# The first MLP product of a decoder layer in pairs of tiles by Strassen's rule, with two sums of weights made by accumulating DMAs

## The chip, the cores and the metric

The kernel runs on one core of a Trainium2 chip. The metric is the device time of one execution in microseconds, the median of 3 runs. The core has TensorE (PE, matrix products, with a weight loader PEld beside it), VectorE (DVE), ScalarE (ACT), GpSimd (POOL), SyncE (SP) and 16 DMA engines. In this kernel SP issues nearly all DMAs; a DMA that POOL issues goes through another queue, called software_dynamic in the profile.

## The reference, cut to what matters

One layer with T=512 tokens, D=2048, D_FF=8192, all in float32. What stands ahead of the second half (an input projection, three mixers, an output projection) is not touched by the change.

```python
x = x + g1 * mix
h = rms_norm(x, norm2_g[l]) * (1.0 + sc2) + sh2
x = x + g2 * (jnp.square(jax.nn.relu(h @ w_mlp1[l])) @ w_mlp2[l])
return rms_norm(x, final_norm_g)
```

Here `sc2`, `sh2` and `g2` are sections of `c_act @ ada_w + ada_b`, vectors of 2048 elements each.

## The kernel before, in words

Every float32 matrix is split into a high part (a cast to the type float32r, on ScalarE) and a low part (the difference, on VectorE). A product of two matrices is three products on TensorE: high by high, low by high, high by low.

The hidden width of 8192 is cut into 64 tiles of 128 rows. The first MLP product `h @ w_mlp1` makes one tile after another, with all 512 tokens as the columns of a matmul. Tiles 0 to 6 are made together in a "wide" phase that goes along the contraction (k = 0 to 15) while `h2`, the normalised input, is still being made. Tiles 7 to 63 come out of `full_k`: 16 steps of k by 3 matmuls of 512 columns, 48 for a tile. Their weights come in four loads of 256 KB a tile through the class `Stream` (tiles `w_raw`), each split into `w_hi` (L135) and `w_lo` (L136).

A tile gets its squared ReLU (`relu2`). After every second tile the four quarters of the two tiles (each 128 x 256) are turned by four subtractions into the seven left factors of a Strassen rule, which the second MLP product uses already: `hx`, 128 x 7 x 256, at L1003 to L1006. They are split into `hx_hi` (L1009) and `hx_lo` (L1010) and written to DRAM in two DMAs of 896 KB (L1012, `hid_dram`). `hx`, `hx_hi` and `hx_lo` have two buffers each.

Between the tiles the kernel fits 16 pieces of `g2` (`ada_piece`: loads of 1 MB and two dots of 128 x 1024 on VectorE, L247), in tiles 7 to 21, and in tiles 8 to 11 `x1_tokens`: 64 transposes on TensorE, 16 copies on ScalarE and 16 DMAs.

Before the last two tiles a pool is closed, and the first two right factors of the second MLP product are loaded ahead, one of them already split. The second MLP product (L1028 to L1031) then takes seven products for each block, with `hs` (left factors) read back from `hid_dram` and `b` (weights, 512 KB a load) split at L975 and L976.

What runs ahead of what on an engine is decided by the order of the program and by the calls `issue_after` and `high_priority`; each engine, SP and POOL too, takes its instructions in order, so one that waits holds up those behind it.

## Time and profile before

| what | value |
|---|---|
| median of 3 runs | 2028.3 us (2026.03 to 2035.21) |
| the profiled execution | 2029.22 us, span 2027.5 us |
| mean granted TensorE clock | 0.994 |
| PE busy | 1981.5 us, 98% of the span, 9141 matmuls |
| DVE busy | 1490.1 us, 73% |
| ACT busy | 844.4 us, 42% |
| POOL busy | 9.8 us |
| DMA | 499.52 MB, mean 246 GB/s |

The share of an engine is an average over stages with different limits; the stretch that the change rewrites is that of tiles 14 to 63, 831.4 to 1385.1 us. The stretch 664.5 to 831.4 us holds the wide phase and tiles 7 to 13.

### The profile page before, as it was taken

To read this page: it belongs to the slowest core of one execution; us is meant where nothing else is said; L and a number is where in the kernel's file an instruction comes from. 1 tells how busy PE (TensorE), PEld (TensorE's weight loads), DVE (VectorE), ACT (ScalarE), POOL (GpSimd) and SP (SyncE) were. 2 spreads that over 40 slices of the span, in tenths; PEclk is the share of its full clock that TensorE was granted. 3 is DMA by queue.
4 is the path that set the end of the run, shared out by engine and by line. 5 is a ranking of instruction groups with operands and counts; after the bars stand their busy time and mean duration, and the time that the engine had idled before them with its cause. 6 is when DMAs were issued, how large, how long until landed. Compare 5 with 4: busy or idle time off the path is not lost.

```text
span 2027.5 us, 25042 instructions
## 1 busy us (share of the span) xinstructions
PE 1981.5 (98%) x9141; PEld 1626.3 (80%) x9141; DVE 1490.1 (73%) x2090; ACT 844.4 (42%) x1258; POOL 9.8 (0%) x17
## 2 busy tenths in 40 slices
PE   9999989999999999999999999999999999999996
PEld 7888977677888887777888888887888887888885
DVE  8998779779987897566444444446887787877778
ACT  5434347776423445323333333334333333433333
...
GB/s 383 296 309 174 247 184 162 182 146 222 273 333 230 92 125 330 278 292 309 216 166 200 179 166 198 180 168 287 333 326 317 309 274 273 345 294 306 310 233 207
DMA packets 217627, 499.52 MB, mean 246 GB/s; under 512 B 16696, under 2 KB 84864, under 8 KB 196640
## 3 DMA queue, kind: packets, MB, share of 16 engines
...
q14 instruction: 51, 0.42, 0.1%
HBM read 430.72 MB, written 67.14 MB: 246 GB/s over the span
## 4 chain that ended last, share of the span: by engine, by line
PE 72%; issue 15%; DMA 6%; DVE 5%; ACT 1%; SPq 0%; POOL 0%; DVEq 0%; ACTq 0%; POOLq 0%
PE ps_m L294 10%; PE ps_m L292 10%; PE ps_m L293 10%; PE ps_w L293 3%; PE ps_w L292 3%; PE ps_w L294 3%; PE ps_rot L1028 3%; PE ps_rot L1029 3%; PE ps_rot L1031 3%; PE ps_d L1031 2%; DMA ada<-in_ada_w 2%; PE ps_d L1028 2%; PE ps_d L1029 2%; PE ps_y L293 1%; PE ps_y L292 1%
## 5 line engine op out<-in xcount | busy, mean ns | idle before, releaser
L135 ACT CAST w_hi<-w_raw 128x512 fp32r<-128x512 f32 (+2 forms) x476 | 285.6, 603 | 582.1 <-PE ps_m L293 329.5
L136 DVE TENSOR_TENSOR w_lo<-w_raw,w_hi 128x512 fp32r<-128x512 f32 (+2 forms) x476 | 315.8, 668 | 260.6 <-ACT w_hi L135 255.9
L294 PE MATMUL ps_m<-h_hi,w_lo 128*128 128x512 f32 x912 | 357.0, 391 | 6.1 <-DVE w_lo L136 6.0
L292 PE MATMUL ps_m<-h_hi,w_hi 128*128 128x512 f32 x912 | 356.6, 391 | 0.0
L293 PE MATMUL ps_m<-h_lo,w_hi 128*128 128x512 f32 x912 | 355.8, 390 | 0.0
L975 ACT CAST v_hi<-b 128x2048 fp32r<-128x2048 f32 x96 | 183.5, 1913 | 299.0 <-PE ps_rot L1029 125.4
L976 DVE TENSOR_TENSOR v_lo<-b,v_hi 128x2048 fp32r<-128x2048 f32 x96 | 219.6, 2290 | 92.2 <-ACT v_hi L975 92.1
L247 DVE SCALAR_TENSOR_TENSOR ada<-ada,crow 128x1024 f32<-128x1024 f32 (+1 forms) x176 | 230.7, 1319 | 42.4 <-DMA ada<-in_ada_w 42.0
L294 PEld LDWEIGHTS ps_m<-h_hi,w_lo 128*128 128x128 f32 x912 | 171.6, 188 | 44.5 <-DVE w_lo L136 8.7
L1028 PE MATMUL ps_rot<-v_hi,hs 128*128 128x512 f32 x512 | 200.5, 392 | 3.8 <-issue 2.3
L292 PEld LDWEIGHTS ps_m<-h_hi,w_hi 128*128 128x128 f32 x912 | 171.7, 188 | 35.4 <-ACT w_hi L135 0.4
L293 PEld LDWEIGHTS ps_m<-h_lo,w_hi 128*128 128x128 f32 x912 | 171.6, 188 | 35.4
L1029 PE MATMUL ps_rot<-v_hi,hs 128*128 128x512 f32 x512 | 199.8, 390 | 0.0
L1028 PE MATMUL ps_d<-v_hi,hs 128*128 128x512 f32 x384 | 149.9, 390 | 4.1 <-DMA hs<-hid_dram 2.6
L1029 PE MATMUL ps_d<-v_hi,hs 128*128 128x512 f32 x384 | 149.4, 389 | 0.0
L1031 PE MATMUL ps_rot<-v_lo,hs 128*128 128x512 f32 x512 | 137.6, 391 | 0.0
L1028 PEld LDWEIGHTS ps_rot<-v_hi,hs 128*128 128x128 f32 x512 | 96.4, 188 | 26.0 <-issue 3.2
L1031 PEld LDWEIGHTS ps_rot<-v_lo,hs 128*128 128x128 f32 x512 | 96.7, 189 | 20.2
L1029 PEld LDWEIGHTS ps_rot<-v_hi,hs 128*128 128x128 f32 x512 | 96.4, 188 | 19.8
L1031 PE MATMUL ps_d<-v_lo,hs 128*128 128x512 f32 x384 | 102.9, 389 | 0.5 <-DVE v_lo L976 0.5
L1055 DVE TENSOR_TENSOR sum<-sum,ps_rot 128x512 f32<-128x512 f32 x112 | 76.2, 683 | 23.8 <-PE ps_rot L1031 23.7
L1028 PEld LDWEIGHTS ps_d<-v_hi,hs 128*128 128x128 f32 x384 | 72.1, 188 | 20.5 <-issue 2.3
...
## 6 DMA issues: line engine op xcount, KB each, us to landing
hs<-hid_dram SPq DMA_DIRECT2D x112, 1024.0 KB, 6.3
w_raw<-in_w SPq DMA_DIRECT2D x412, 256.0 KB, 3.1
b<-in_w SPq DMA_DIRECT2D x128, 512.0 KB, 6.6
...
ada<-in_ada_w SPq DMA_DIRECT2D x92, 512.0 KB, 5.0
hid_dram<-hx_hi SPq DMA_DIRECT2D x32, 896.0 KB, 4.8
hid_dram<-hx_lo SPq DMA_DIRECT2D x32, 896.0 KB, 5.2
...
```

The costliest lines, as they stand in the source:

```text
L135: self.split = nc.scalar.copy(hi, raw)
L136: self.in_order(lambda: nc.vector.tensor_sub(lo, raw, hi.bitcast(F32)))
L247: return V.scalar_tensor_tensor(w, w, 0.5, crow[:, sl], ALU.mult, ALU.mult, accum_out=acc[:, n:n + 1])
L292: PE.matmul(ps, lhsT=wh, rhs=pair[0], start=first, stop=False)
L293: PE.matmul(ps, lhsT=wh, rhs=pair[1], start=False, stop=False)
L294: PE.matmul(ps, lhsT=wl, rhs=pair[0], start=False, stop=last)
L975: S.copy(hi, raw)
L976: V.tensor_sub(lo, raw, hi.bitcast(F32))
L1028: PE.matmul(ps, lhsT=hs[:, 0, k, ts], rhs=hi[:, k], start=(first and k == 0), stop=False)
L1029: PE.matmul(ps, lhsT=hs[:, 1, k, ts], rhs=hi[:, k], start=False, stop=False)
L1031: PE.matmul(ps, lhsT=hs[:, 0, k, ts], rhs=lo[:, k], start=False, stop=(last and k == KP - 1))
L1055: V.tensor_add(d, d, s)
```

## The change: what it does

`N0 = 14`: tiles 0 to 13 are made as before, and tiles 14 to 63 in 25 pairs. A pair of tiles by 512 tokens by 2048 of contraction is cut in two in each of the three directions, and the two-by-two block product is made by 7 products instead of 8. One of them (`up_product`) is 8 steps of k (128 each) by 3 matmuls of 256 columns: 24 matmuls, 168 a pair, where a pair had 96 of 512 columns. The right-hand operands are halves of `h2` or sums of them (`next_sums`, 8 groups of 4 subtractions, 2 casts and 2 differences, made once, during tiles 8 and 9). The left-hand operands are quarters of the weights (512 KB each) or sums of them: `w22`, `w11` and `w21` are loaded by SP; `q4 = w12 + w22` and `q5 = w12 + w11` are each made by a plain DMA and an accumulating DMA on top of it, both issued by POOL; `w11 + q4` and `w21 + w11` are additions of 128 x 1024 on VectorE. Each of the 7 left-hand operands is split (128 x 1024, L1135 and L1136); the splits run two products ahead, with three buffers. The four quarters of the result are put together from the 7 sums in PSUM: two copies on ScalarE into `z3` (L1186, L1188) and four operations of 512 elements on VectorE (L1191, L1193, L1194, L1197), and ReLU and square are now two operations on ScalarE.

With it go other edits. Weight buffers (`w22`, `w11`, `w21`, `q4`, `q5`), `hx`, `hx_hi` and `z3` have one buffer each in the pair stage; the low part is written over `hx` itself (L1027). `h2` is computed in place on `x1`, so `x1_tokens` moves ahead into the wide phase. Of the 16 pieces of `g2`, 4 go into the wide phase, and the other 12 into 24 halves, one a pair (load L1170, dot L262). Nothing of the second MLP product is split or loaded before the pools of the pairs close; its first three splits stand behind them.

```diff
-    x = None
-    for n in range(NFT):
-        if n == NFT - 2:
-            groups_scope.close()
...
-            ahead.append(split(*next(todo)))
-            second = next(todo)
...
+        hi, lo = sums_hi[k], low.pop(0)
+        a, b = [x1[i // 4][:, i % 4] for i in (k, k + KH)]
+        h11, h21, h12, h22 = a[:, :HT], a[:, HT:], b[:, :HT], b[:, HT:]
+        V.tensor_sub(h11, h12, h11)
+        V.tensor_sub(h12, h12, h22)
+        V.tensor_sub(h22, h22, h11)
+        V.tensor_sub(h21, h21, h22)
+        for i, x in enumerate((a, b)):
+            S.copy(hi[:, i], x)
+            V.tensor_sub(lo[:, i], x, hi[:, i].bitcast(F32))
...
+    def w1_load(t, i, key, more=None):
+        t2 = t.rearrange("p (c t) -> p c t", c=2)
+        (G if more else nc.sync).dma_start(t2, w1_block(i, key))
+        if more:
+            G.dma_start(t2, w1_block(i, more), accum_op=ALU.add)
...
+        two_blocks(5, N0 // 2, "12", "22")
+        two_blocks(6, N0 // 2, "12", "11")
+        w22, w11, q4, w21, q5 = [pair_raw[m] for m in (3, 2, 5, 4, 6)]
+        for i in range(N0 // 2, NFT // 2):
+            w1_load(w22, i, "22")
+            yield i, 3, w22
+            w1_load(w11, i, "11")
+            yield i, 2, w11
+            yield i, 5, q4
+            V.tensor_add(w11, w11, q4)
+            two_blocks(5, i + 1, "12", "22")
+            yield i, 1, w11
+            w1_load(w21, i, "21")
+            yield i, 4, w21
+            V.tensor_add(w21, w21, w11)
+            yield i, 7, w21
+            yield i, 6, q5
+            two_blocks(6, i + 1, "12", "11")
...
+    def w1_split(i, m, raw):
+        nonlocal splits
+        hi, lo = pair_hi[splits % 3], pair_lo[splits % 3]
+        splits += 1
+        S.copy(hi, raw)
+        ws.last = V.tensor_sub(lo, raw, hi.bitcast(F32))
+        return i, m, hi, lo
...
+    def up_product(ps, m, hi, lo):
+        for k in range(KH):
+            ks = slice(k * P, (k + 1) * P)
+            xh, xl = left(m, k)
+            PE.matmul(ps, lhsT=hi[:, ks], rhs=xh, start=(k == 0), stop=False)
+            PE.matmul(ps, lhsT=hi[:, ks], rhs=xl, start=False, stop=False)
+        for k in range(KH):
+            PE.matmul(ps, lhsT=lo[:, k * P:(k + 1) * P], rhs=left(m, k)[0], start=False, stop=(k == KH - 1))
...
+        for m in (3, 2, 5, 1, 4, 7, 6):
+            _, _, hi, lo = ahead1.pop(0)
+            up_product(bank[m], m, hi, lo)
+            if m == 2:
+                S.copy(z3[:, 1], bank[2])
+            elif m == 5:
+                S.copy(z3[:, 0:3:2], four[:, 1:2].to_broadcast([P, 2, HT]))
+            elif m == 4:
+                x = hidden(i)
+                V.tensor_add(x[:, 1:6:4], z3[:, 1:3], four[:, 0:4:3])
+                z = z3[:, 0:2]
+                V.tensor_sub(z, four[:, 0:4:3], z)
+                V.tensor_add(z, z, one.to_broadcast([P, 2, HT]))
+                square(x[:, 1:6:4], x[:, 1:6:4])
+            elif m == 6:
+                V.tensor_add(x[:, 0:7:6], z, two)
+                square(x[:, 0:7:6], x[:, 0:7:6])
...
+        left_factors(i, x)
...
+    for _ in range(3):
+        ahead.append(split(*next(todo)))
```

Three places show how the instructions stand. The first is VectorE around the end of a pair of tiles. Before, `w_lo` are low parts of the coming tile's weights, L893 is the square of the ReLU, `hx23` holds the factors of tiles 46 and 47:

```order
L136 TENSOR_TENSOR w_lo414_10720<-w_raw_414_10717,w_hi414_10719 128x512
L893 TENSOR_TENSOR hx23_10628<-hx23_10628 128x512
L1003 TENSOR_TENSOR hx23_10628<-hx23_10628 128x256
L1004 TENSOR_TENSOR hx23_10628<-hx23_10628 128x256
L1005 TENSOR_TENSOR hx23_10628<-hx23_10628 128x256
L1006 TENSOR_TENSOR hx23_10628<-hx23_10628 128x256
L136 TENSOR_TENSOR w_lo415_10738<-w_raw_415_10735,w_hi415_10737 128x512
L1010 TENSOR_TENSOR hx_lo23_10711<-hx23_10628,hx_hi23_10710 128x1792
```

Now, at the same place for pair 17 (`pair_l0` to `pair_l2` are the three buffers of low parts, of the weights that the next pair uses; `w1_raw` holds w22 and w11, `pair_5` is q4, `pair_4` is w21, `ps_z17` the banks of pair 17):

```order
L1191 TENSOR_TENSOR hx17_10311<-pair_z_7998,ps_z17_4_10173 128x2x256
L1136 TENSOR_TENSOR pair_l1_7997<-pair_5_7993,pair_h1_7996 128x1024
L1193 TENSOR_TENSOR pair_z_7998<-ps_z17_4_10173,pair_z_7998 128x512
L1194 TENSOR_TENSOR pair_z_7998<-pair_z_7998,ps_z17_1_10175 128x512
L1197 TENSOR_TENSOR hx17_10311<-pair_z_7998,ps_z17_2_10174 128x2x256
L1136 TENSOR_TENSOR pair_l2_8000<-w1_raw_7992,pair_h2_7999 128x1024
L1020 TENSOR_TENSOR hx17_10311<-hx17_10311 128x256
L1021 TENSOR_TENSOR hx17_10311<-hx17_10311 128x256
L1022 TENSOR_TENSOR hx17_10311<-hx17_10311 128x256
L1136 TENSOR_TENSOR pair_l0_7995<-pair_4_8001,pair_h0_7994 128x1024
L1023 TENSOR_TENSOR hx17_10311<-hx17_10311 128x256
L1124 TENSOR_TENSOR pair_4_8001<-pair_4_8001,w1_raw_7992 128x1024
```

Behind these stand L1027 (the low part of `hx17`, 1792 elements, written over it) and the low part for m=7, from `pair_4`. What has moved: the combining and the factors of one pair stand among the low parts of the next one, and the first row, L1191, writes the single buffer `hx`, so it waits until the DMA of pair 16's low part has left it.

The second place is SP's queue in the same stage. Before, `w_raw` are weight loads, `hid_dram5` the writes of the factors:

```order
L125 DMA w_raw_393_10288<-in_w 128x512
L125 DMA w_raw_394_10310<-in_w 128x512
L1012 DMA hid_dram5_7127<-hx_hi20_10227 128x7x256
L125 DMA w_raw_395_10328<-in_w 128x512
L1012 DMA hid_dram5_7127<-hx_lo20_10228 128x7x256
L125 DMA w_raw_396_10346<-in_w 128x512
```

Now one pair has six DMAs on SP (`w1_raw` is w22 in the first row and w11 in the third; `hx16` in the last row is its low part):

```order
L1099 DMA w1_raw_7992<-in_w 128x2x512
L1170 DMA g2_w_8013<-in_ada_w 128x1024
L1099 DMA w1_raw_7992<-in_w 128x2x512
L1029 DMA hid_dram4_7298<-hx_hi16_10168 128x7x256
L1099 DMA pair_4_8001<-in_w 128x2x512
L1029 DMA hid_dram4_7298<-hx16_10095 128x7x256
```

What has moved: the write of the low part stands behind the load of w21, which waits until VectorE has read w21 of the pair before for m=7. POOL, which had no DMA in this stage, now has four a pair, in the order q4 plain, q4 accumulating, q5 plain, q5 accumulating; each accumulating one waits at the queue's head until its plain one has landed.

The third place is SP at the end of the stage. Before, the loads of the second MLP product (`b21`, `b22`, with left factors `hs0`) stand ahead of the last writes:

```order
L1012 DMA hid_dram7_7129<-hx_lo30_11838 128x7x256
L921 DMA b21_0_0_12037<-in_w 128x2x512 x2
L969 DMA hs0_0_6_12040<-hid_dram0_7122 128x2048
L921 DMA b22_0_0_12052<-in_w 128x2x512 x2
L1012 DMA hid_dram7_7129<-hx_hi31_12010 128x7x256
L1012 DMA hid_dram7_7129<-hx_lo31_12011 128x7x256
```

Now:

```order
L1029 DMA hid_dram7_7301<-hx30_13119 128x7x256
L952 DMA b11_0_0_13439<-in_w 128x2x512 x2
L1000 DMA hs0_0_1_13442<-hid_dram0_7294 128x2048
L952 DMA b12_0_0_13448<-in_w 128x2x512 x2
L1000 DMA hs0_0_4_13453<-hid_dram0_7294 128x2048
L1029 DMA hid_dram7_7301<-hx_hi31_13397 128x7x256
```

What has moved: the first factor `b11` (and its `hs0`, both laid over areas that the pair stage has used) is only loaded here, and before it was loaded and split earlier.

## Rows read from the trace of the kernel before

**Rows 1.** The page's part 1: busy us, share of the span, instructions.

```profile
PE 1981.5 (98%) x9141; PEld 1626.3 (80%) x9141; DVE 1490.1 (73%) x2090; ACT 844.4 (42%) x1258; POOL 9.8 (0%) x17
```

**Rows 2.** By stretch: us, PE, PEld, DVE, ACT, POOL (count), clock, DMA share, GB/s.

```profile
664.50:744.20 79.70, 79.70 (x368) 66.47 (x366) 67.62 (x113) 36.48 (x62) 0.00 (x0) 1.00 0.34 96
744.20:831.40 87.20, 84.75 (x402) 69.06 (x402) 62.73 (x99) 41.95 (x61) 0.00 (x0) 1.00 0.87 290
831.40:1385.10 553.70, 547.54 (x2400) 450.84 (x2400) 283.18 (x419) 190.94 (x275) 0.00 (x0) 1.00 0.64 209
1385.10:1650.00 264.90, 261.82 (x1151) 215.50 (x1151) 211.01 (x132) 101.63 (x60) 0.00 (x0) 1.00 0.89 324
```

**Rows 3.** Timeline of TensorE: start us, us, then the instruction; four tile starts.

```profile
831.44 0.39 PE L292 MATMUL ps_m<-h_hi,w_hi 128*128 128x512 f32 x1
...
1211.29 0.39 PE L292 MATMUL ps_m<-h_hi,w_hi 128*128 128x512 f32 x1
...
1222.17 0.39 PE L292 MATMUL ps_m<-h_hi,w_hi 128*128 128x512 f32 x1
...
1385.37 0.39 PE L1028 MATMUL ps_rot<-v_hi,hs 128*128 128x512 f32 x1
```

**Rows 4.** Timeline of TensorE in the input projection, matmuls of 384 and 272 columns.

```profile
215.79 0.33 PE L536 MATMUL ps_tm<-w_hi,h_lo 128*128 128x384 f32 x1
...
216.31 0.33 PE L536 MATMUL ps_tm<-w_hi,h_lo 128*128 128x384 f32 x1
...
220.72 0.28 PE L534 MATMUL ps_tm<-w_hi,h_hi 128*128 128x272 f32 x1
...
222.47 0.29 PE L536 MATMUL ps_tm<-w_hi,h_lo 128*128 128x272 f32 x1
```

**Rows 5.** Groups by line of VectorE, by shape: busy us, mean ns | idle before.

```profile
L247 DVE SCALAR_TENSOR_TENSOR ada<-ada,crow 128x1024 f32<-128x1024 f32 x160 | 194.1, 1222 | 42.3 <-DMA ada<-in_ada_w 42.0
L1055 DVE TENSOR_TENSOR sum<-sum,ps_rot 128x512 f32<-128x512 f32 x112 | 76.2, 683 | 23.8 <-PE ps_rot L1031 23.7
L1010 DVE TENSOR_TENSOR hx_lo<-hx,hx_hi 128x1792 fp32r<-128x1792 f32 x32 | 64.8, 2025 | 29.8 <-ACT hx_hi L1009 29.8
L1003 DVE TENSOR_TENSOR hx<-hx 128x256 f32<-128x256 f32 x32 | 13.6, 425 | 0.9
L1073 DVE TENSOR_TENSOR sum<-sum,g2row 128x1024 f32<-128x1024 f32 x6 | 7.2, 1220 | 0.0
```

**Rows 6.** Groups by line of ScalarE, by shape.

```profile
L135 ACT CAST w_hi<-w_raw 128x512 fp32r<-128x512 f32 x412 | 255.2, 620 | 533.3 <-PE ps_m L293 318.4 <-PE ps_w L293 88.6 <-DMA w_raw<-in_w 55.2
L1009 ACT CAST hx_hi<-hx 128x1792 fp32r<-128x1792 f32 x32 | 54.3, 1696 | 35.3 <-DVE hx L1006 35.3
```

**Rows 7.** DMA from 1211 to 1374 us: queue, then issues with median us to landing.

```profile
q1 hardware_dynamic: 22236, 29.36, 56.6%
w_raw<-in_w SPq DMA_DIRECT2D x59, 256.0 KB, 2.7
hid_dram<-hx_lo SPq DMA_DIRECT2D x8, 896.0 KB, 5.1
```

**Rows 8.** DMA from 1700 to 1710 us, with one accumulating DMA of POOL.

```profile
q0 software_dynamic: 272, 0.52, 32.8%
c<-x_dram POOLq DMA_DIRECT2D x1, 512.0 KB, 6.2
```

**Rows 9.** DMA from 1714 to 1720 us: accumulating and other issues.

```profile
sum<-x_dram POOLq DMA_DIRECT2D x2, 512.0 KB, 10.8
b<-in_w SPq DMA_DIRECT2D x2, 512.0 KB, 10.5
```

**Rows 10.** The page's part 6: weight loads of 512 KB, median us to landing.

```profile
b<-in_w SPq DMA_DIRECT2D x128, 512.0 KB, 6.6
```

**Rows 11.** Tiles 7 to 21 of the first product: what TensorE waited for.

```profile
  DVE w_lo L136: 14.2, 10
```

**Rows 12.** Weight loads of one matmul form, by line.

```profile
L292 PEld LDWEIGHTS ps_m<-h_hi,w_hi 128*128 128x128 f32 x912 | 171.7, 188 | 35.4 <-ACT w_hi L135 0.4
```

More of the change, by code (lines that the diff above doesn't have):

```diff
@@ L26 @@
 NCK = NFT // (2 * KP)
+KH = KT // 2
+N0 = 14
 GELU_C = 0.7978845608028654
@@ L1013, in trunk_kernel, with next_sums @@
-    ada_some(len(ada_todo))
-    mlp_scope.close()
-    work_scope.close()
-    pools["now"] = ctx.enter_context(tc.tile_pool(name="w2b", bufs=1, reuse_waits="tile"))
+        for part, y in enumerate((hi.bitcast(F32), x)):
+            nc.sync.dma_start(hid_dram[i // KP][:, :, part, i % KP].rearrange("i p t -> p i t"), y)
+    h2_sums = {}
+    low = []
+    sums_hi = [sum_pool.tile([P, 2, T], F32R, name=f"h2s_hi{k}") for k in range(KH)]
+    def next_sums():
+        if len(h2_sums) == KH:
+            return
+        k = KH - 1 - len(h2_sums)
+        if not low:
+            if k in (5, 4):
+                low.append(groups.tile([P, 2, T], F32R, tag="ada", bufs=2, name=f"h2s_lo{k}"))
+            else:
+                two = groups.tile([P, 4, T], F32R, tag="p8", bufs=5, name=f"h2s_lo{k}")
+                low.extend((two[:, :2], two[:, 2:]))
+        hi, lo = sums_hi[k], low.pop(0)
[8 more added lines that the diff above has]
+            V.tensor_sub(lo[:, i], x, hi[:, i].bitcast(F32))
+        h2_sums[k] = {m: [y[:, i, j:j + HT] for y in (hi, lo)] for m, i, j in ((3, 0, 0), (6, 0, HT), (7, 1, 0), (1, 1, HT))}
@@ new lines, in trunk_kernel @@
+    x = None
+    for n in range(N0):
+        if n < 7:
+            ps, cols = banks[n], shb2[:, n, 0:1]
+        else:
+            ps, cols = mm_bank(f"ps_m{n}"), None
+            full_k(ps, h2, (), next_sums if n > 7 else None)
+        if n % 2 == 0:
+            x = hidden(n // 2)
+            relu2(halves(x, 0), ps, cols)
+            continue
+        relu2(halves(x, 5), ps, cols)
+        left_factors(n // 2, x)
+    burst_scope.close()
+    main_scope.close()
+    pairs_scope = ExitStack()
@@ new lines, in trunk_kernel, with g2_load, g2_dot @@
+    todo1 = w1_factors()
+    with tc.high_priority():
+        ahead1 = [w1_split(*next(todo1)) for _ in range(2)]
+    g2_todo = [(n, h) for n in ada_todo for h in range(2)]
+    g2_rows = group4("g2_w").rearrange("p c t -> p (c t)").rearrange("p (h n) -> p h n", h=2)
+    g2_in = []
+    def g2_load():
+        n, h = g2_todo.pop(0)
+        nc.sync.dma_start(g2_rows[:, h], a["ada_w"][n][:, h * 1024:(h + 1) * 1024])
+        g2_in.append((n, h))
+    def g2_dot():
+        n, h = g2_in.pop(0)
+        ada_dot(g2_rows[:, h], n, (modh, mod)[h], h)
@@ new lines, in trunk_kernel @@
+    for i in range(N0 // 2, NFT // 2):
+        four = psum.tile([P, 4, HT], F32, tag="four", bufs=2, name=f"ps_z{i}_4")
+        two = psum.tile([P, 2, HT], F32, tag="two", bufs=2, name=f"ps_z{i}_2")
+        one = psum.tile([P, 1, HT], F32, tag="one", bufs=2, name=f"ps_z{i}_1")
+        bank = {4: four[:, 0], 5: four[:, 1], 2: four[:, 2], 3: four[:, 3], 7: two[:, 0], 6: two[:, 1], 1: one[:, 0]}
+        for m in (3, 2, 5, 1, 4, 7, 6):
[15 more added lines that the diff above has]
+                square(x[:, 0:7:6], x[:, 0:7:6])
+            with tc.high_priority():
+                y = next(todo1, None)
+                if y:
+                    ahead1.append(w1_split(*y))
+                with tc.issue_after(ws.last.ins):
+                    if m == 4 and g2_in:
+                        g2_dot()
+                    if m == 7 and g2_todo:
+                        g2_load()
+        left_factors(i, x)
```

153 lines of the change are left out of this document (104 added, 49 removed).

## The prediction

> **What bounds the kernel now.** First the busy times of the engines: TensorE is busy for 1981.5 us, 98% of the span, VectorE for 73%, ScalarE for 42% [rows 1]. The reader is to see that only TensorE is close to the span, so a change gains by giving TensorE less time. An average hides stages, so next the same by stretch [rows 2]. In the stretch that the change rewrites, 831.4 to 1385.1 us, TensorE is busy for 547.5 of 553.7 us, VectorE for 283.2 (51%), ScalarE for 190.9 (34%), the DMA engines for 64%, at a granted clock of 1.00, the upper of the two levels (2.4 GHz). Three resources have room there, TensorE none.
>
> Then the timeline [rows 3]: a tile goes from 1211.29 to 1222.17, 10.88 us for 48 matmuls, 226.7 ns from start to start. A pair of tiles takes 21.76 us. Fifty tiles would be 544 us; from the start of tile 14 at 831.44 to the first matmul of the second product at 1385.37 are 553.9. So some 10 us are stalls. What tiles 7 to 21 wait for is mostly the low part of a weight split, 14.2 us in 10 waits [rows 11], in the tiles that carry the pieces of `g2`.
>
> **The change part by part.**
>
> *TensorE.* Per pair it removes 96 matmuls of 512 columns and adds 168 of 256. No row has 256 columns with float32r operands, but matmuls of 384 take (216.31 - 215.79) / 3 = 173 ns from start to start, and 14 steps of 272 take 222.47 - 220.72 = 1.75 us, 125 ns each [rows 4]. From 512 to 384 to 272 the slope is 0.42 ns a column each time, so the time follows the columns without a floor showing, and 256 gives 118.2 ns. 168 x 118.2 = 19.86 us a pair, 1.9 less than 21.76. That is the best that the stage can do.
>
> *VectorE.* A subtraction of 128 x 1024 takes 1.22 us, of 512 about 0.685, of 256 0.425, of 1792 2.03, a dot of 1024 1.22 [rows 5]. Per pair: 7 low parts (8.54), 2 additions (2.44), 4 combinations (2.74), 4 subtractions for the left factors (1.70), L1027 (2.03) and the dot of `g2` (1.22) are 18.7 us, where two tiles took 283.2 / 553.7 x 21.76 = 11.1. That is 94% of the new floor of TensorE: under it, but with nothing to spare for a wait.
>
> *ScalarE.* A cast of 512 takes 0.62 us, of 1792 1.70 [rows 6], so 0.84 ns an element and 1.05 us for 1024. Seven of these, the two copies into `z3` (0.4 and 0.6), four activations of 512 (2.5) and the cast of the factors (1.7) are 12.5 us. Not a bound.
>
> *DMA.* Plain bytes per pair: five blocks of weights by 0.524 MB, the two writes of factors 1.835 MB, and 0.524 MB for `g2`, 4.98 MB in all. In quiet tiles 29.36 MB took 56.6% of 163 us, 318 GB/s at full share [rows 7]; in the second product 324 GB/s came at a share of 0.89, 364 GB/s [rows 2]. So 13.7 to 15.7 us of all 16 engines. An accumulating DMA of 0.5 MB took 32.8% of 10 us, 3.28 us, twice a plain one [rows 8]; two are 6.6 us. Sum: 20.2 to 22.2 us a pair, where it was 57% of 21.76. So the DMA engines become as full as TensorE.
>
> *The loop through the one buffer `hx`.* L1191 of a pair waits until the DMA of the low part of the pair before has left `hx`. In VectorE's order from L1191 to that DMA stand L1191, the low part for m=5, L1193, L1194 and L1197, the low part for m=1, three subtractions, the low part for m=4, the fourth, L1124, L1027 and the low part for m=7, for which SP's load of w21 waits ahead of the DMA: 0.69 + 1.22 + 2.06 + 1.22 + 1.28 + 1.22 + 0.43 + 1.22 + 2.03 + 1.22 = 12.6 us, and some 0.5 for the cast ahead of L1027, 13.1. Then the DMA itself: 5.1 us to land when alone [rows 7], and 512 KB of w21 ahead of it and 512 KB of POOL beside it, 1.4 us each at 364 GB/s: 7.9. The loop is 21.0 us. While L1191 waits, the low parts of the next three products are queued behind it on VectorE, and TensorE waits for those.
>
> *POOL.* The single buffer q4 is free after L1119, then comes a load, then its accumulation, then cast and low part: (load + accumulation) + 2.9 has to fit into a pair, so the two must take under 18 us. Loads of 512 KB take 6.6 us in the median [rows 10], 10.5 in a crowd, accumulations 6.2 alone [rows 8] and 10.8 in a crowd [rows 9]. 13 to 17 us fit, 21 don't.
>
> So a pair lasts at least 19.86 (TensorE); by the loop 21.0; by the DMA engines 20.2 to 22.2, in the middle 21.2. I take 21.0, between TensorE's and the upper DMA figure.
>
> *Start and end.* The first q4 is needed two products (5.7 us) after the first pair begins; load, accumulation and split take 2.7 [rows 7] + 6.2 + 2.3 = 11.2 us from when its area comes free: nothing if that is one tile earlier, 5.5 us if at tile 13's end. I take 2. At the end the first factor `b11` was split long ahead; now its area is released during the fifth of the last pair's seven products, some 7.1 us before TensorE is done, and load (6.6 [rows 10]), cast of 2048 (1.9) and low part (2.3, both by the slopes above) are 10.8: 3.7 us late, with the later factors behind it. I take 3.5.
>
> *Tiles 0 to 13* (664.5 to 831.4 us, 166.9 us). VectorE has 67.6 + 62.7 = 130.3 us of work there [rows 2]. Out go some 8 pieces of `g2` of tiles 7 to 13 (2.44 us each, -19.5), in come 4 in the wide phase (+9.8) and the 8 sums (4 x 0.425 + 2 x 0.685 = 3.07 each, +24.6): 145 us, 87%. The moved transposes cost TensorE the same in either place. I cost this at nothing, since VectorE still has 22 us spare; without that cover it is up to +7, and if the stalls on low parts shrink, up to -5 (half of tiles 7 to 13's share of the 14.2).
>
> *The sum.* Pairs 25 x 21.0 = 525, start and end 5.5: 530.5 us against 553.9, 23.4 less. The profiled execution took 2029.2 us (span 2027.5 and 1.7 around it), 0.9 above the median, which is left aside: 2029.2 - 23.4 = **2006 us**.
>
> **A rule weighed.** POOL issues four DMAs a pair here and issued none in this stage before; the rows of its DMAs are 6.2 us alone and 10.8 in a crowd. The Trainium skill, DMA: Bandwidth & Descriptors, "Anatomy of one DMA — SWDGE (gpsimd) path", fits such a DMA as 2.0 us and the bytes at 436 GB/s, an estimate of 3.2 us for 512 KB; by it a load and its accumulation would be over in 6.4 us, POOL would never be late and the forecast would be the same or lower. The rows differ by two to three times, for the accumulating kind, and the rows decide.
>
> **The rivals.**
>
> *A, TensorE alone sets the pace.* If the DMA of the low part lands sooner (its loop has 14.2 us of TensorE's five products from L1197 on to fit into) and the DMA engines reach 364 GB/s, a pair takes 19.9. For it: VectorE at 94% and DMA at 20.2 just fit. Against: three resources would have to run between 94% and 102%. 25 x 19.9 + 5.5 = 503, 2029.2 - 553.9 + 503 = 1978 us.
>
> *B, no gain.* Either the DMA engines need the upper 22.2 us, or matmuls of 256 columns don't cost 118 ns: one with a weight load each could be held by the load, whose row has 188 ns [rows 12], overlapped. At 130 ns a pair would be 21.84. Against the second: 272 columns, with a load each, went at 125 ns [rows 4]. A pair of 21.9: 553, 2028 us. That is also the case that the change doesn't do what it says.
>
> *C, slower by the DMA engines.* They did not pass a share of 0.89 in the second product [rows 2], where loads and writes are as dense as they would be here. 20.2 / 0.89 = 22.7 us a pair, 573 in all: 2048 us. It decides from 21.9 a pair on, a share of 0.92.
>
> *D, slower by POOL's chain.* If load and accumulation each take the 10.8 us of the crowd [rows 9], the loop is 21.6 + 2.9 = 24.5 us a pair, 618 in all: 2093 us. It decides from 19 us for the two. For it: the DMA engines are crowded throughout. Against: in the quiet row it is 6.2. The Trainium skill, SBUF — State Buffer, "🔬 SBUF: two separate sides", says that VectorE can keep POOL from writing its DMA's descriptors; no row here shows it, and it would act on the same chain.
>
> **How the numbers follow.** Chances: the forecast 0.43, A 0.22, B 0.13, C 0.13, D 0.09. A measurement of this kernel tells 0.5% (10 us) from no change. Faster are the forecast and A, 0.65; the same is B, 0.13; slower are C and D, 0.22. The range reaches from A with the 5 us that tiles 0 to 13 may give, rounded, 1974, to C, 2048: only D and half of C and a little below A lie outside. The forecast's own range, for pairs of 20.4 to 21.5, is 1991 to 2019.
>
> **What would show it.** Steps of matmuls of 256 columns of 118 ns in a product without waits; more than that, and B is right. A pair to pair time on TensorE's timeline near 21.0 with stalls that VectorE's low parts release, and on VectorE a wait ahead of L1191 for the DMA of `hx`: my loop. No stalls and 19.9: A. A DMA share of 0.95 and over with 21 a pair, or of 0.89 with 22.7: C. Waits of L1119 or of the low part for m=5 or m=6 for the accumulating DMA: D. The prediction would be wrong above all if the accumulating DMAs, of which the trace before shows only a few, cost more among dense traffic than the one row shows, or if the first split of the second product came much later than 3.5 us.

## The result, and the profile after

The changed kernel takes 2080.84 us in the median of 4 runs (2077.02 to 2083.31), the kernel before 2029.46 (2026.03 to 2035.21) in runs beside it: ratio 1.0249, 95% interval 1.0219 to 1.0278. Slower by 51 us, where 23 us faster was forecast. The profiled execution has a span of 2081.6 us; before it was 2027.5.

The page's part 1, after (busy us, share of the span, instructions), answers to [rows 1]:

```profile
PE 1976.5 (95%) x10941; PEld 1704.9 (82%) x10941; DVE 1671.0 (80%) x2213; ACT 969.8 (47%) x1365; POOL 106.5 (5%) x117
```

TensorE is busy hardly less than before, although its work fell. The timeline of TensorE shows where the 54.1 us of the span went. The first pair starts at 833.31, where tile 14 started at 831.44 [rows 3]: 1.9. From there to the first matmul of the second product, 1425.67, are 592.4 us, where there were 553.9: 38.4 more. From that matmul to the end of the span are 655.9 us, where there were 642.1: 13.8 more.

Four starts on that timeline (start us, us, instruction, idle before):

```profile
1079.01 0.28 PE L1151 MATMUL ps_z<-h_hi,pair_h 128*128 128x256 f32 x1
...
1080.43 0.28 PE L1151 MATMUL ps_z<-h_hi,pair_h 128*128 128x256 f32 x1
...
1103.53 0.58 PE L1151 MATMUL ps_z<-h_hi,pair_h 128*128 128x256 f32 x1 [2.58 <-ACT pair_z L1186]
...
1425.67 0.47 PE L1233 MATMUL ps_rot<-v_hi,hs 128*128 128x512 f32 x1 [1.54 <-DMA hs<-hid_dram]
```

The first two are 12 steps apart: 118.3 ns each, so the matmuls of 256 columns cost what was forecast, and 25 pairs of 168 need 497 us. The rest of the stage is waits, and steps at a lower clock behind them. The list of waits, 833 to 1420 us (engine, line, what for: us, times, longest; a PEld row is the same wait as the PE row with its names, seen by the weight loader, and isn't added to it):

```profile
POOL pair L1101 <- DMA pair<-in_w: 278.2, 49, 8.6
POOL pair L1099 <- DVE pair_l L1136: 198.7, 46, 8.4
ACT pair_h L1135 <- PE ps_z L1152: 117.7, 83, 1.8
ACT hx L1157 <- DVE hx L1191: 59.6, 23, 5.6
DVE pair_l L1136 <- ACT pair_h L1135: 57.9, 49, 4.8
DVE hx L1191 <- DMA hid_dram<-hx: 50.7, 17, 5.2
PEld ps_z L1151 <- ACT pair_z L1186: 41.0, 20, 4.0
...
PE ps_z L1151 <- ACT pair_z L1186: 36.8, 19, 3.8
```

The first two rows are POOL's own. L1101 issues the accumulating DMA and waits for the plain one to land. L1099 issues the plain one and has to wait for a free buffer 46 times, so POOL is ahead of the engines that it serves. One cycle shows how the others hang together. VectorE, SP and ScalarE by timeline:

```profile
1072.22 0.68 DVE L1191 TENSOR_TENSOR hx<-pair_z,ps_z 128x512 f32<-128x512 f32 x1
...
1082.06 2.03 DVE L1027 TENSOR_TENSOR hx<-hx,hx_hi 128x1792 fp32r<-128x1792 f32 x1 [0.67 <-ACT hx_hi L1026]
...
1097.08 0.69 DVE L1191 TENSOR_TENSOR hx<-pair_z,ps_z 128x512 f32<-128x512 f32 x1 [4.70 <-DMA hid_dram<-hx]
```

```profile
1085.25 0.37 SPq L1099 DMA_DIRECT2D pair<-in_w  x1
1085.96 0.83 SPq L1029 DMA_DIRECT2D hid_dram<-hx  x1
```

```profile
1097.80 0.63 ACT L1157 ACTIVATE hx<-hx 128x512 f32<-128x512 f32 x1 [5.08 <-DVE hx L1191]
...
1099.00 1.03 ACT L1135 CAST pair_h<-w_raw 128x1024 fp32r<-128x1024 f32 x1
...
1102.18 1.03 ACT L1135 CAST pair_h<-pair 128x1024 fp32r<-128x1024 f32 x1
1103.11 0.36 ACT L1186 COPY pair_z<-ps_z 128x256 f32<-128x256 f32 x1
```

From L1191 to the issue of the write of `hx` are 13.7 us, the write lands 11.1 later (1097.08), and only then the next L1191 goes: a loop of 24.9 us. Behind L1191 stand, on ScalarE in this order, the ReLU (L1157), the cast for product 1, the cast for product 4 and the copy L1186. TensorE waits twice for them: for the cast, and then, five matmuls into product 1, for the copy (1103.53). The copy reads product 2, product 5 goes into another quarter of the same PSUM tile `four`, and its first matmul waits until the copy is done. Over the stage TensorE waits 36.8 us for this copy and 18.0 for casts; the prediction had it wait for VectorE's low parts, behind L1191.

Windows of 2 us of the same cycle (us, PE, PEld, DVE, ACT, POOL busy (count), granted clock, DMA share, GB/s):

```profile
1098.00:1100.00 2.00, 0.27 (x3) 0.07 (x1) 1.97 (x3) 1.97 (x3) 0.76 (x1) 1.00 0.99 188
1100.00:1102.00 2.00, 0.86 (x5) 0.66 (x5) 1.97 (x3) 1.01 (x3) 0.00 (x0) 1.00 0.68 178
1102.00:1104.00 2.00, 0.47 (x2) 0.47 (x3) 1.71 (x5) 1.48 (x3) 0.34 (x1) 0.65 0.26 104
1104.00:1106.00 2.00, 2.00 (x11) 2.00 (x11) 2.00 (x3) 0.81 (x1) 0.84 (x1) 0.50 0.24 20
...
1110.00:1112.00 2.00, 2.00 (x19) 2.00 (x18) 0.68 (x2) 1.05 (x1) 0.00 (x0) 1.00 1.02 359
```

In the 6 us from 1098 to 1104 TensorE is busy for 1.6; in the last 2 of them the granted clock falls to the lower level (0.50, 1.2 GHz), and it is back at 1.00 in the last row. So a wait is paid again afterwards. Of all starts in the stage, 41 are more than 0.3 us behind the one before and exceed 118.5 ns by 62.6 us in all; 308 are 0.16 to 0.3 us behind, 29.2 us in all, of which 26.2 lie in the stretches at the lower clock. Together 92 of the stage's 95 us above 497. Most pairs that wait last 25 to 28 us, most of those between 20 to 22, and the mean is 23.7.

The DMA engines from 833 to 1425 us (queue: packets, MB, share; issues: KB, median us to landing):

```profile
q1 hardware_dynamic: 69330, 97.84, 46.8%
q0 software_dynamic: 20613, 51.73, 38.7%
...
hid_dram<-hx SPq DMA_DIRECT2D x25, 896.0 KB, 10.4
```

46.8 + 38.7% of 592 us are 20.2 us a pair, the lower of the two figures forecast. The write that was put at 7.9 us takes 10.4 in the median.

The end: windows at the start of the second product (columns as above):

```profile
1426.00:1436.00 10.00, 8.27 (x37) 6.48 (x36) 9.19 (x8) 4.75 (x5) 0.00 (x0) 1.00 0.85 311
1436.00:1446.00 10.00, 6.05 (x22) 4.57 (x21) 2.73 (x2) 2.35 (x2) 0.00 (x0) 0.90 1.06 412
1446.00:1456.00 10.00, 8.62 (x35) 6.54 (x34) 10.00 (x5) 6.33 (x5) 0.00 (x0) 0.93 0.83 317
```

TensorE is idle 7.1 of these 30 us; in the first 30 us of the second product before it was 3.0. From 1425 us to the end it waits 10.8 us for left factors that are read back (`hs`), where it was 2.6 before, and 1.7 for the cast of a weight. The DMA engines are full in the middle row (1.06; a transfer is counted where it starts, so a short window can pass 1). What the rest of the 13.8 us is, was not followed further.

### The profile page after: what moved, and what is told of

It reads as the page before. It is cut to its first block, busy times and chain, and to the rows that moved or that the text cites. A ratio compares the mean times of both kernels' runs of the same rounds, so it can differ in the third digit from the quotient of the medians.

```text
span 2081.6 us, 28742 instructions
## 1 busy us (share of the span) xinstructions
PE 1976.5 (95%) x10941; PEld 1704.9 (82%) x10941; DVE 1671.0 (80%) x2213; ACT 969.8 (47%) x1365; POOL 106.5 (5%) x117
## 4 chain that ended last, share of the span: by engine, by line
PE 55%; issue 15%; DMA 15%; DVE 11%; ACT 3%; SPq 0%; POOL 0%; DVEq 0%; ACTq 0%; POOLq 0%
DMA hid_dram<-hx 8%; PE ps_z L1151 4%; PE ps_z L1152 3%; PE ps_z L1154 3%; PE ps_w L308 3%; PE ps_w L307 3%; PE ps_w L309 3%; PE ps_rot L1233 2%; PE ps_rot L1236 2%; PE ps_rot L1234 2%; PE ps_d L1236 2%; PE ps_d L1233 2%; PE ps_d L1234 2%; DVE pair_l L1136 2%; PE ps_m L309 2%
## 5 line engine op out<-in xcount | busy, mean ns | idle before, releaser
L144 ACT CAST w_hi<-w_raw 128x512 fp32r<-128x512 f32 (+2 forms) x276 | 160.7, 587 | 235.0 <-PE ps_w L308 72.1
L1151 PE MATMUL ps_z<-h2s_hi,pair_h 128*128 128x256 f32 x800 | 197.7, 284 | 18.1 <-ACT pair_h L1135 18.0
L1233 PE MATMUL ps_rot<-v_hi,hs 128*128 128x512 f32 x512 | 201.7, 394 | 10.5 <-DMA hs<-hid_dram 6.9
L145 DVE TENSOR_TENSOR w_lo<-w_raw,w_hi 128x512 fp32r<-128x512 f32 (+2 forms) x276 | 177.1, 648 | 41.1 <-ACT w_hi L144 40.1
L262 DVE SCALAR_TENSOR_TENSOR ada<-ada,crow 128x1024 f32<-128x1024 f32 (+1 forms) x152 | 200.6, 1329 | 9.7 <-DMA ada<-in_ada_w 9.6
L1151 PE MATMUL ps_z<-h_hi,pair_h 128*128 128x256 f32 x600 | 165.6, 308 | 37.0 <-ACT pair_z L1186 36.8
L1152 PE MATMUL ps_z<-h2s_lo,pair_h 128*128 128x256 f32 x800 | 196.8, 283 | 0.0
L1151 PEld LDWEIGHTS ps_z<-h2s_hi,pair_h 128*128 128x128 f32 x800 | 152.0, 190 | 20.4 <-ACT pair_h L1135 20.4
L1152 PE MATMUL ps_z<-h_lo,pair_h 128*128 128x256 f32 x600 | 162.6, 303 | 0.0
L1151 PEld LDWEIGHTS ps_z<-h_hi,pair_h 128*128 128x128 f32 x600 | 126.1, 210 | 41.5 <-ACT pair_z L1186 41.0
L1152 PEld LDWEIGHTS ps_z<-h2s_lo,pair_h 128*128 128x128 f32 x800 | 152.4, 190 | 0.0
L1136 DVE TENSOR_TENSOR pair_l<-pair,pair_h 128x1024 fp32r<-128x1024 f32 x100 | 120.9, 1219 | 18.8 <-ACT pair_h L1135 16.4
L1135 ACT CAST pair_h<-pair 128x1024 fp32r<-128x1024 f32 x100 | 104.5, 1045 | 58.9 <-PE ps_z L1152 54.6
L1152 PEld LDWEIGHTS ps_z<-h_lo,pair_h 128*128 128x128 f32 x600 | 126.7, 211 | 0.0
L1136 DVE TENSOR_TENSOR pair_l<-w_raw,pair_h 128x1024 fp32r<-128x1024 f32 x75 | 91.6, 1221 | 43.6 <-ACT pair_h L1135 41.7
```

The source lines that it names most:

```text
L144: self.split = nc.scalar.copy(hi, raw)
L145: self.in_order(lambda: nc.vector.tensor_sub(lo, raw, hi.bitcast(F32)))
L262: return V.scalar_tensor_tensor(w, w, 0.5, crow[:, sl], ALU.mult, ALU.mult, accum_out=acc[:, n:n + 1])
L1135: S.copy(hi, raw)
L1136: ws.last = V.tensor_sub(lo, raw, hi.bitcast(F32))
L1151: PE.matmul(ps, lhsT=hi[:, ks], rhs=xh, start=(k == 0), stop=False)
```

## The experiments

The theories: **H**, the loop through `hx` sets the pace; **C** (O in the first expectation), TensorE's order and its wait for ScalarE's copy; **D**, the work of the DMA engines, POOL's chain or the supply of weights, with the wait for `hx` only taking up slack. Ratios are to the kernel before, with their 95% intervals.

### The order, and the copy

e1 holds the products in order, by `issue_after` on the last matmul of the product before.

```diff
+        if last_mm:
+            with tc.issue_after(last_mm.pop()):
+                up_matmuls(ps, m, hi, lo)
```

> One edit: each product's matmuls are held behind the last matmul of the product before, so that the five matmuls of product 1 no longer stand ahead of product 5 on TensorE; VectorE's order moves L1191 ahead of the low parts for m=2 with it. Theory H (the write of the low part holds the one buffer hx; VectorE, ScalarE and then TensorE wait behind L1191): the loop through hx keeps its length (24.9 us when it waits), so the gain is small, a pair of 23 to 24 us, 2065 to 2085 us. Theory O (what costs is that TensorE needs the high part for m=1 one product early, while its cast stands behind the ReLU of the late L1191): the late L1191 is covered by 2.85 us more, most stalls and the low clock after them go, a pair of 21 to 22 us, 2025 to 2050 us.

2096.67 us, ratio 1.0319 (1.0298 to 1.034). VectorE's wait for `hx` is nearly gone (2.5 us), and the time is longer: TensorE waits for the copy in every pair, 60.2 us in 25 waits. Neither theory came out as stated.

e3 and e4 keep that order, leave the 24 loads and dots of `g2` out (12 of the 16 pieces of that gate are missing), and e4 has a second `hx` in their memory.

```diff
+        if i >= 8 and i % 2 == 0:
+            return hx_b
```

> Products in order as in the first run, and the 24 loads and dots of g2 in the pairs left out (12 columns of the gate are zero). DMA falls by 1.4 us a pair, VectorE by 1.2. It is the control for the next run. Theory H: still a wait of L1191 for the write of the low part, a pair of 21.5 to 23 us, 2035 to 2070 us. Theory D (the DMA engines' share sets the pace): 23.7 x (20.4 - 1.4) / 20.4 = 22.1 us a pair, 2040 us.

> As the control (g2 in the pairs left out, products in order, the same order of instructions on every engine), with a second buffer for hx in the space of the g2 loads. Theory H: no wait of L1191 for a DMA, a pair of 19.9 to 20.5 us, 1985 to 2005 us. Theory D: the same time as the control within 10 us, since the same bytes move. Theory O alone: the same as the control.

2095.7 (1.0311) and 2095.59 (1.0313): no difference. In both, TensorE waits for the copy in all 25 pairs, and nearly all of them last 24.0 us. This said nothing on H.

e5 gives product 2 a place in product 1's PSUM tile and product 5 a tile of its own; e7 is e5 without those loads and dots of `g2`, e8 is e7 with two `hx`.

```diff
+        five = psum.tile([P, 1, HT], F32, tag="five", bufs=2, name=f"ps_z{i}_5")
...
+        one = psum.tile([P, 2, HT], F32, tag="one", bufs=2, name=f"ps_z{i}_1")
+        bank = {4: four[:, 0], 5: five[:, 0], 2: one[:, 1], 3: four[:, 1], 7: two[:, 0], 6: two[:, 1], 1: one[:, 0]}
```

> One edit against the changed kernel: the seven sums of a pair lie in other PSUM tiles (4 and 3 in one, 5 in one of its own, 1 and 2 in one, 7 and 6 in one), so that the first matmul of product 5 no longer waits for ScalarE's copy of product 2 out of the same tile. VectorE's, ScalarE's and the queues' orders stay word for word; TensorE takes the products in the order 3, 2, 5, 1 again by itself. Theory C (TensorE's stalls are that copy, which stands on ScalarE behind the ReLU of a late L1191): the 37 us of idle time at product 5 and most of the 29 us at the lower clock behind it go, a pair of 20.8 to 21.8 us, 2010 to 2035 us. Theory H (the write of the low part out of the one hx): the wait of L1191 stays and now ends in the low part for m=5 and the cast for m=1, which stand behind it; 23 to 24 us a pair, 2065 to 2085 us.

> The new PSUM tiles with the loads and dots of g2 in the pairs left out (12 columns of the gate are zero); VectorE's order is that of the earlier run without g2. It is the control for the next run. Theory C: the 24 us a pair of the earlier run without g2 fall to 20 to 21, 1990 to 2015 us. Theory H: 2060 to 2095 us.

> As the control, with a second buffer for hx in the space of the g2 loads; all orders are the control's. Theory H, as a second limit behind theory C: 10 to 25 us less than the control, pairs of 19.9 to 20.2 us. Theory C alone: within 6 us of the control.

2076.43 (1.0224; 1.0202 to 1.0247), 2071.05 (1.0192; 1.0163 to 1.0221) and 2058.13 (1.0143; 1.0117 to 1.0168). The wait for the copy moved to product 1, which now shares the tile; the second `hx` gave 13 us, and what was left was again the copy (41 us on TensorE) and casts that wait for loads.

e9 gives products 2 and 5 a tile each. The orders of VectorE, ScalarE and the queues in the pairs are as they were, but for one copy in the first pairs; on TensorE the five matmuls of product 1 no longer stand ahead of product 5.

> One edit against the changed kernel: product 2 and product 5 get a PSUM tile of their own each, so that no matmul waits for a copy of another product's sum any more (in the last runs without that wait at product 5 it had come back at product 1). VectorE's, ScalarE's and the queues' orders stay word for word. Theory C (the wait for the copies is what TensorE loses): 20.5 to 21.5 us a pair, 2005 to 2030 us. Theory D (the loads and writes of a pair land late, since the DMA engines are 86% busy and what they carry comes in one burst; the waits only show it): the stalls go over to the casts and low parts, 23 to 23.6 us a pair, 2065 to 2080 us.

2074.11 (1.0221; 1.0204 to 1.0237). The clock is 0.99 again, the wait for the copy gone, and 7 us gained, which the two intervals don't quite tell apart. TensorE still loses 63.7 us in starts of more than 0.3 us behind, as much as in the changed kernel, but in shorter pieces: 2 of 67 are over 2 us, where it was 17 of 41, and the clock no longer falls within the pairs. The list of waits of e9, VectorE:

```profile
DVE hx L1193 <- DMA hid_dram<-hx: 93.5, 24, 5.4
DVE hx L1027 <- ACT hx_hi L1026: 16.5, 23, 1.8
```

The wait for `hx` nearly doubled (50.7 in the changed kernel). So the copy and the low clock were what the loop through `hx` looked like on TensorE: C falls as the cause of most of the time.

### The work of the DMA engines

e2 leaves the accumulating DMAs out (`q4` and `q5` are `w12` alone), e6 does so with e5's tiles.

> Leaves out the two accumulating DMAs of each pair (q4 and q5 are then w12 alone); all orders on the engines stay. The DMA engines lose 6.4 us of 20.4 a pair. Theory D (the DMA engines or POOL's chain set the pace): a pair falls to 20 to 20.5 us and the time to 1985 to 2000 us. Theory H: the low part's write lands in 6 to 7 instead of 10.4 us, so the loop through hx falls from 24.9 to about 21 us, and a pair to 20.5 to 21.5: 2000 to 2030 us. If neither the engines' load nor the landing matters: 2075 to 2085 us.

> The same with the two accumulating DMAs of a pair left out (q4 and q5 are w12 alone). Theory C with the DMA engines as what makes L1191 late: no stall is left in the pairs, 20.0 to 20.3 us each, 1985 to 2000 us. If the DMA engines don't matter: the time of the run before.

2027.33 (0.9983; 0.996 to 1.0005) and 2025.66 (0.9981; 0.9963 to 1.0), medians of 10 runs that lie between 2017 and 2037. The write of `hx` lands in 7.2 us, and the share of q0, POOL's queue, is 13.1%. So a plain load of POOL takes 13.1% of 567 us, 74 us over 49 loads, 1.5 us of all engines. In the changed kernel 38.7% of 592 us are 229, for 49.4 loads of each kind, and an accumulating one takes (229 - 74) / 49.4 = 3.1; the prediction had 3.28. e10 puts a plain DMA of the same bytes in its place (`q4` and `q5` hold the second block alone):

```diff
-            G.dma_start(t2, w1_block(i, more), accum_op=ALU.add)
+            G.dma_start(t2, w1_block(i, more))
```

> The changed kernel with the accumulating DMA replaced by a plain DMA of the same bytes on the same queue with the same waits (q4 and q5 are then w22 and w11). Left out is the addition alone. If what costs is the time of the DMA engines (3.1 us for an accumulating DMA, 1.4 for a plain one of 512 KB, so 3.3 us a pair less): a pair of 21 to 22 us, 2030 to 2050 us, nearer to the run without accumulation (2027) than to the changed kernel (2081). If what costs is POOL's chain of two DMAs in a row per sum: within 10 us of 2081.

2051.65 (1.0117; 1.01 to 1.0134): 29 us are gained, with a landing of 9.0 us:

```profile
hid_dram<-hx SPq DMA_DIRECT2D x25, 896.0 KB, 9.0
```

POOL's chain has as many steps as before, but its DMAs land in 4.4 us where they took 6.4, so by itself this run doesn't rule the chain out. The waits of the changed kernel do: POOL has 198.7 us to spare for free buffers, and VectorE and ScalarE wait 6.6 us in all, in 3 waits, for anything loaded into `q4`, `q5` or `w21`. So POOL's chain isn't it, and the DMA engines' work counts; by way of what, the mean times on the timeline from 900 to 1340 us tell (the landing is the median of the stage; L1191 stands for the first write of `hx` in each kernel, whatever its line):

| kernel | L1191 to issue of its write | landing (median) | sum | L1191 to L1191 |
|---|---|---|---|---|
| changed | 13.6 | 10.4 | 24.0 | 23.8 |
| e9 | 13.5 | 9.5 | 23.0 | 23.4 |
| e10 | 13.5 | 9.0 | 22.5 | 22.5 |
| e2 | 13.5 | 7.2 | 20.7 | 21.5 |
| e17 (below) | 12.5 | 6.3 | 18.8 | 20.3 |

In the first three the loop is the pace, within 0.4 us. In the last two the sum is 0.8 and 1.5 us below the period, which is near TensorE's 19.9 there. (e2's trace is of the slowest of its ten runs, 2036.66 us.)

e11 and e12 load `w12` once and make the sums on VectorE or on GpSimd, with e9's tiles.

```diff
+            V.tensor_add(w22, w22, w12)
+            yield i, 5, w22
+            V.tensor_add(w12, w12, w11)
```

> The PSUM tiles of the first run of this batch, and no accumulating DMA: w12 is loaded once a pair by SP (two buffers), q4 = w22 + w12 and q5 = w12 + w11 are two more additions on VectorE, in place; the result is the reference's. DMA falls from 20.4 to about 12.5 us a pair, VectorE rises from 18.7 to 21.1. Theory D: VectorE is the next bound, 21.2 to 22 us a pair, 2015 to 2040 us. Theory C or H (the queues and the buffer of hx as such): no gain over the first run of this batch, or slower by VectorE.

> The same with the two additions on GpSimd, which is idle otherwise. Theory D: VectorE back at 18.7 us a pair, 20 to 21.5 us a pair, 1990 to 2020 us, if an addition of 128 x 1024 takes GpSimd under 5 us and doesn't slow VectorE; if GpSimd is slower than that, or holds VectorE up, slower than the run before.

2097.33 (1.0345; 1.0329 to 1.0362) and 2061.68 (1.0165; 1.015 to 1.018). With the sums on VectorE the DMA engines' share falls to 0.55 and the write lands in 4.5 us, but from the first write of `hx` to the issue of the DMA are 18.0 us instead of 13.5 (TensorE waits for L1194, 62.5 us), and the time is longer. So the DMA engines' work alone doesn't set the pace. With GpSimd 12 us are gained over e9, and the casts wait for the sums. Both missed their forecasts: here the work could not simply be moved to another engine's queue.

### Two tiles `hx` without the wait for the copy

e13 is e9 without those loads and dots of `g2`; e14 has two `hx` beside.

> Control for the next run: products 2 and 5 have PSUM tiles of their own, and the 8 pieces of the last gate's weights that the stage loads and multiplies are left out (so that gate is wrong). Theory H (the loop through the one tile hx, VectorE's work on it 12 to 14 us and the landing of its write 8 to 10 us, sets the pace of a pair): 2065 to 2074 us, since a third of the pairs only lose a 1 MB load beside the hx write; VectorE still waits for that write in most pairs, pair 22.5 to 23. Theory D (the DMA engines' total work sets the pace): 1 MB less in a pair of three is 1 us a pair, 2048 us.

> The control's kernel with a second tile hx for every other pair, in the memory that the left-out weights had; the same instructions in the same order. Theory H: VectorE's wait for the write of hx is gone, the pair falls from about 23 to 20.0 to 20.8 us, the time by 2.3 times 25 = 55 us, to about 2010 (1995 to 2025). Theory D (DMA work, or the casts and loads of weights, set the pace and the wait for hx only takes up the slack): within 10 us of the control, the waits come back at the casts for their weights.

The stage loads 12 pieces in 24 halves of 512 KB, not 8 of 1 MB as these expectations say. 2065.1 (1.018; 1.0161 to 1.0198) and 2053.06 (1.0108; 1.0086 to 1.0131). The wait for `hx`, 85.1 us on VectorE in e13, is gone, and 12 us are gained, not 55. A second loop takes over: the cast's wait for a weight load, first in the changed kernel, then in e14.

```profile
ACT pair_h L1135 <- DMA w_raw<-in_w: 6.5, 2, 3.7
```

```profile
ACT pair_h L1137 <- DMA w_raw<-in_w: 74.4, 20, 5.6
```

Timeline of e14, VectorE, SP and ScalarE:

```profile
1083.93 1.23 DVE L1121 TENSOR_TENSOR w_raw<-w_raw,pair 128x1024 f32<-128x1024 f32 x1
...
1091.73 2.03 DVE L1029 TENSOR_TENSOR hx<-hx,hx_hi 128x1792 fp32r<-128x1792 f32 x1 [1.80 <-ACT hx_hi L1028]
...
1094.92 1.22 DVE L1126 TENSOR_TENSOR pair<-pair,w_raw 128x1024 f32<-128x1024 f32 x1
...
1106.72 1.22 DVE L1121 TENSOR_TENSOR w_raw<-w_raw,pair 128x1024 f32<-128x1024 f32 x1
```

```profile
1096.17 0.37 SPq L1101 DMA_DIRECT2D w_raw<-in_w  x1
```

```profile
1104.38 1.05 ACT L1137 CAST pair_h<-w_raw 128x1024 fp32r<-128x1024 f32 x1 [3.97 <-DMA w_raw<-in_w]
```

`w11` has one buffer too. It is last read by L1126 (`w21 + w11`), which stands on VectorE behind the whole low part of `hx`; then comes its load, 8.2 us to the cast, cast, low part and L1121: 22.8 us from L1121 to L1121, 22.7 in the mean from 900 to 1340 us. Both loops run through the same piece of VectorE's queue, with the 1.8 us wait for the cast of all of `hx` in it. H had the sign right and not the size, and D described what came next.

e16 keeps `g2`, moves its 12 pieces to the stage before, and has e14's two `hx`. Other than its expectation says, it adds the half sums and the bias of that gate twice, two small additions (128 x 16) more than the reference needs.

```diff
-    ada_left = (NFT - N0) // 4
+    ada_left = 0
```

> Computes all of the reference: the 8 pieces of the last gate's weights move from this stage to the one before it, and a second whole tile hx stands where they were. Theory H: the pair as in the run with two tiles (20.0 to 20.8), and the stage before longer by what its 8 MB more of loads and 8 dots of VectorE cost there, of the order of 8 times 2 us; 2010 to 2035. Theory D: 2060 to 2080.

2088.19 (1.0291; 1.0271 to 1.0311): the pairs begin at 861.45 us, where it is 831.94 in e14. The moved loads and dots cost 29.5 us there, and nothing is gained in the pairs over e14 (570.4 us from the first pair to the second product, against 567.1).

### The low part in two

e15 has e9's PSUM tiles, orders `hx` as four quarters and three sums, casts the quarters while VectorE still makes the sums, makes the low parts in two steps and writes them in two DMAs; the quarters have a second buffer in half of the `g2` buffer. e17 takes that second buffer away, e18 gives products 2 and 5 their shared tile back.

```diff
+        for x, js in parts:
+            S.copy(hi[:, js], x)
+        write(0, slice(0, 7), hi.bitcast(F32))
+        for x, js in parts:
+            V.tensor_sub(x.bitcast(F32R), x, hi[:, js].bitcast(F32))
+            write(1, js, x)
```

> Computes all of the reference: the four quarters of hx in two buffers (the second in half of the gate's weight buffer, whose loads then go through the other half), the three sums of them in one; two casts and two writes of the low part in place of one. Theory H: the second buffer lets the first add of the next pair go ahead of the write, so the loop is only 4 to 5 us of VectorE's and ScalarE's work on the three sums plus a landing; pair 20.5 to 21.5, time 2015 to 2035. Theory D: as without it, 2065 to 2080.

> The version at 2007 us with one thing undone: all pairs put their quarters into hx itself, so there is one buffer again; the casts, the low parts and the two writes stay split, and the rows of the engines stand in the same order but for one low part of weights. Theory H (the loop through one buffer of hx sets the pace): VectorE's wait for the write of hx comes back, pair 22 to 23.5 us, 2050 to 2080. Theory D (it was the order and the split of the low part's work that helped, not the buffer): 2005 to 2020.

> The version at 2007 us with the other thing undone: products 2 and 5 back in the PSUM tile that they share with 3 and 4, as in the changed kernel; the scheduler then puts five matmuls of product 1 ahead of product 5 again. Theory H: the copy's wait was only late because of the loop; with two buffers for the quarters it costs 0 to 1.5 us a pair, 2005 to 2045. Theory C (TensorE's wait for ScalarE's copy of product 2 and the low clock behind it is a cost of its own): pair 21.5 to 23, 2045 to 2085.

| | shared PSUM tile | own tiles |
|---|---|---|
| `hx` written whole | changed kernel: 1.0249 (1.0219 to 1.0278) | e9: 1.0221 (1.0204 to 1.0237) |
| in two parts | e18: 2020.15, 0.994 (0.9925 to 0.9955) | e15: 2007.08, 0.9888 (0.9862 to 0.9914); e17: 2006.82, 0.9877 (0.9854 to 0.9901) |

All three beat both kernels. The second buffer, which H had asked for, gives nothing (e17 against e15); the two parts, with the order that comes with them, give 67 us with own tiles (2074.1 against 2006.8). The timeline of e17, VectorE and SP:

```profile
1076.91 0.68 DVE L1206 TENSOR_TENSOR hx<-pair_z,ps_z 128x512 f32<-128x512 f32 x1
...
1088.47 2.09 DVE L1039 TENSOR_TENSOR hx<-hx,hx_hi 128x1024 fp32r<-128x1024 f32 x2
...
1097.50 0.68 DVE L1206 TENSOR_TENSOR hx<-pair_z,ps_z 128x512 f32<-128x512 f32 x1
```

```profile
1089.73 0.52 SPq L1033 DMA_DIRECT2D hid_dram<-hx  x1
```

Its waits, DMA issues and the window, 833 to 1385 us (which takes in the first 34 us of the second product), and its first matmul of the second product:

```profile
DVE hx L1025 <- DMA hid_dram<-hx: 1.3, 2, 1.0
```

```profile
hid_dram<-hx SPq DMA_DIRECT2D x26, 512.0 KB, 6.3
...
hid_dram<-hx SPq DMA_DIRECT2D x26, 384.0 KB, 9.1
```

```profile
833.00:1385.00 552.00, 533.54 (x4310) 525.13 (x4309) 471.10 (x540) 316.46 (x387) 95.10 (x98) 0.98 0.99 297
```

```profile
1351.21 0.77 PE L1248 MATMUL ps_rot<-v_hi,hs 128*128 128x512 f32 x1 [7.94 <-DMA hs<-hid_dram]
```

Next pair's first add (L1206) overwrites quarters alone, so it waits for the 512 KB that were written first: issued 1 us earlier in the loop, landing 6.3 us later. The loop is 18.8 us, below TensorE's 19.9, and the wait is gone. The low part no longer waits for a cast, so `w11`'s loop is shorter too: from its first write to its last read are 9.4 us in most pairs, 11.0 in e14. A pair takes 20.4 us (from 833.66 to 1351.21, less 7.9 of wait at the end, over 25), with the DMA engines at a share of 0.99. The first pair takes 26.5 us, the others 20.1 in the mean. e17 makes every DMA that e2 leaves out and is 20 us faster than e2, so the amount of DMA work by itself was no limit here. Taking the first loop away by itself gave 12 us (e14), shortening both gave 67; no run shortens the second alone, and how much of the gain is the order and how much the smaller write isn't separated.

## Why the prediction was wrong

- **TensorE, 118.2 ns a matmul, floor 19.86.** Right: 118.3 ns, and in e15's profiled run, the fastest of its four, the pairs behind the first take 19.97 in the mean.
- **DMA engines, 20.2 to 22.2 us a pair.** Right at the lower end, 20.2, with 3.1 us for an accumulating DMA.
- **The loop through `hx`, 13.1 + 7.9 = 21.0.** The step that failed. The mechanism was right as far as it went: the loop sets the pace, by the wait that was named (50.7 us in 17 pairs). VectorE's part was 13.6. The landing of the write was mis-sized: the 7.9 came from a quiet stretch with two transfers added, and it measured 10.4 among dense traffic; a stretch with such traffic stood in [rows 9], 10.5 us for 512 KB, and wasn't used for it. Loop 24.0, pair 23.7; 592.4 us for the stage against 525 forecast is 67 of the 77.5 us between forecast and result (23.4 less forecast, 54.1 more in the span). Nor does the prediction have a loop through the one buffer of `w11`: it is 22.7 us in e14, so with the wait for `hx` away a pair still doesn't come down to 21.0 in that traffic (22.6 behind the first).
- **What is behind the wait.** Not seen: that product 5 waits for ScalarE's copy out of the same PSUM tile, with that copy behind the ReLU on ScalarE, and that the clock falls in the wait. In the changed kernel this is a part of the price of the loop's lateness; with the split, where the loop no longer waits, it is 13 us, with the order of the matmuls that comes with it (e18 against e15).
- **Start, 2 us, and tiles 0 to 13, nothing.** Tiles 0 to 13 lose 1.9 us. POOL issues the first load of q4 at 830.67, only 2.6 us before the first pair begins: nearly the case that was put at 5.5 us and weighed down to 2. TensorE waits 5.7 us for a cast in the first pair, which takes 28.4 us, 4.7 above the mean. The 2.7 us in that sum is the row of a 256 KB load, and q4's load is of 512 KB.
- **End, 3.5 us.** Mis-sized: 13.8 us. The prediction took the split of the first weight to be late and the rest to follow at its old pace; here TensorE waits mostly for left factors read back, 10.8 us, beside full DMA engines. e17 keeps this loss (655.1 us behind the pairs) and has 7.9 us of the same wait just ahead of it. No run changed the end by itself.
- **POOL's chain (D).** The time, 2081, is nearest to this rival's 2093, but not by its mechanism: POOL waits 198.7 us for free buffers, and VectorE and ScalarE hardly wait for its sums. The Trainium skill, DMA: Bandwidth & Descriptors, "Anatomy of one DMA — SWDGE (gpsimd) path", fits a DMA of POOL as 2.0 us and the bytes at 436 GB/s, an estimate of 3.2 us for 512 KB; POOL's DMAs here, plain and accumulating, land in 6.4 in the median, so the measurement is twice the estimate, but it made no difference to the time.
- **C, a cap of 0.89 on the DMA share.** There is no such cap: e17 runs at 0.99 with pairs of 20.4. The 0.89 was a mean over 264.9 us, and the first 18.6 us of that stretch had 0.99.
- **A and B** did not occur in the changed kernel; A's pair of 19.9 occurs in e15, with the DMA engines at a share of 1.00 from 833 to 1380 us.
